# Silu, the key map and the final state on ScalarE, requests a tile ahead and fewer stored halves in a hybrid short-convolution / HGRN2 layer

## The chip, the cores and the metric

The kernel runs on one core of a Trainium2 chip. The metric is the device time of one execution in microseconds. PE is TensorE (matmuls), ACT is ScalarE, DVE is VectorE, POOL is GpSimd and SP is the engine whose queue issues most DMAs (GpSimd's queue issues the rest). In the code they are `T`, `A`, `V`, `G` and `SP`.

## The reference, cut to what matters

One layer runs over a prompt of 2048 tokens and a sample of 64, 1024 features each, in fp32.

```python
h = rms_norm(x, g_pre)
vA, bA, cA, zA, q, f, iv, zB, gA, gB = split_cols(einsum('btd,dn->btn', h, w_in))
u = cA * vA                                             # path A
yA = (silu(zA) * bA * causal_conv3(u, conv_w)) @ w_a_out
fg = lb + (1 - lb) * sigmoid(f)                         # path B: 8 heads of 128
logf, kk, qq = log(fg), 1 - fg, silu(q) * QK_SCALE
S_new, o = hgrn2_scan(S0, qq, kk, iv, logf)             # chunks of 64 tokens
o = o * rsqrt(mean(o * o) + EPS) * g_onorm
yB = (o * silu(zB)) @ w_b_out
out = (sigmoid(gA) * yA + sigmoid(gB) * yB) @ w_o
x = x + rms_norm(out, g_post)
gate = sigmoid(rms_norm(x, g_ple) @ w_ple_gate)
x = x + (p @ w_ple_proj) * gate
```

The outputs are x for both runs, the last two columns of u (the convolution's history) and the final state of each head.

## The kernel before, in words

The 2112 tokens (prompt, sample inside it, prompt) are cut into three blocks of 704 columns; a half is 352 columns. Activations lie with features on the 128 partitions, so one tile is 128 x 704. `rt()` hands out such tiles from a ring of 52, `hf()` tiles of half the width from 9.

Every product is made of three matmuls of 128 x 128 by 352 columns: an operand is split into a high half `hi`, made by a cast on ScalarE, and a low half `lo`, made by a subtraction on VectorE (`split`, L183), and hi·hi, hi·lo and lo·hi are added in PSUM. Weights come from `w_blk` in halves of 256 KB: `load_raw` (L192) asks SP's queue for one, `split_w` (L209) makes `hi` (4 buffers) and `lo`. In the first use of a weight the low half is stored to DRAM (L221); later uses load it (L215) and make only `hi` anew. `load_w` (L224) does this for the two halves of a 1024 x 128 weight column group. Groups 80 to 87 are W_A (`w_a_out`), 88 to 95 W_B, 96 to 103 W_O, 104 to 111 W_G (`w_ple_gate`).

Most of the input projection goes through `sgroup` (L343): two column groups at once by seven block products instead of eight (a Strassen scheme, table at L67), each product 12 matmuls (L357 to L359), in PSUM banks a, c, d, b from a pool of 5. Copies (L371), additions (L377, L382) and a caller's `sink` empty the banks; a sink's `whole` (L391, addition at L396) and `into` (L399, addition at L403) join two partial results. The banks are used again by the next group, so PE waits where a bank's last reader is late.

The stages of a block:

- Path B: for each head `head_prep` (L809) makes forget gates, queries, decays, keys, values and `z` from two `sgroup` calls. `sink_f` stores the sigmoid of f in `sf` and the queries in `qe`. Then come a sigmoid of the queries (L824), the logarithm (L826), the query product (L827), the key map 1 - fg (L828), the scan, and, inside the second group, `scaled`: three exponentials (L840 to L842) and the products with them (L843 to L857). `sink_v` (L859) makes `vt` and `z`. `head_attn` (L873) does the attention of a head; its steps run as hooks between the products of later groups. L942 scales the state at the end of a run.
- Gates, and path A: `path_a` (L751), with `sink_z` for silu(zA) · the rest.
- Merge: block 0 in `merge` (L1048), by `gemm` over `load_w` column groups; blocks 1 and 2 in `merge_in_turn` (L1082), which walks block products over all groups. It names `anew=("A11", "A12")` for W_A and W_B, so of `w_blk` only the second half of groups 4 to 7 (block A22) uses a stored low half there; `out_in_turn` (L1129) has `anew=()` for W_O.
- Final: `final_out`, `final_norm` (L1141; squares L632/L633, column sums on PE L614, transposes L598, x_fm loads L1153), then the gate. `final_gate` (L1185) runs for blocks 0 and 1, inside the first stage of block 1 and the last stage of block 2. It multiplies W_G group j, reloads the tiles `x` and `p` which were put away in DRAM (`reload`, L1041, on POOL's queue), takes the sigmoid (L1191), multiplies and adds (L1192, L1193) and stores y_fm (L1194). Block 2 uses `gate_in_turn` (L1209) at the very end.

A scheduler sets the order of instructions on each engine from the written order, priorities (`tc.high_priority`) and `tc.issue_after`; each engine then executes in that order, and POOL issues its DMAs in order among its other work. In the profile the groups of instructions are named by line, and L184 is the `split` of whatever calls it.

Of the kernel before, what the change touches and what calls it, by code (L numbers as in the profile page):

```python
# [23 lines left out]
CH = 64  # L24
# [58 lines left out]
def hybrid_step(  # L83
# [140 lines left out]
    def load_w(idx, anew=False):  # L224

        parts = []
        for half_ in range(2):
            raw = load_raw(w_blk[idx, half_])
            with tc.high_priority():
                parts.append(split_w(raw, None if anew else (idx, half_)))  # L230
        return parts
# [156 lines left out]
    def half(t, h):  # L388
        return t[:, h * HN : (h + 1) * HN]
# [361 lines left out]
    def path_a(bl, hc, a, first, extra, ready=None):  # L751

        for j in range(KB):
# [36 lines left out]
            def sink_z(c, h, x, y):  # L790
                if c == 1:
                    into(half(b, h), x, y)
                else:
                    v = whole(x, y)
                    A.activation(half(z, h), v, AF.Sigmoid)
                    V.tensor_tensor(half(z, h), v, half(z, h), ALU.mult)

# [11 lines left out]
    def head_prep(bl, hc, hd, first, hs):  # L809
        n, npair = bl["n"], bl["npair"]  # L810
        nch, np1 = n // CH, npair * P
        sf, qe, sq = rt(), rt(), rt()

# [8 lines left out]
        else:  # L822
            sgroup(FF * 8 + hd, QQ * 8 + hd, hc, sink_f, first)
        A.activation(sq, qe, AF.Sigmoid)  # L824
        lg, b, eq = rt(), rt(), rt()
        A.activation(lg, sf, AF.Ln, bias=lb[:, hd : hd + 1], scale=omlb[:, hd : hd + 1])  # L826
        V.scalar_tensor_tensor(qe, qe, QK_SCALE, sq, ALU.mult, ALU.mult)  # L827
        V.tensor_scalar(sf, sf, nomlb[:, hd : hd + 1], omlb[:, hd : hd + 1], ALU.mult, ALU.add)  # L828
        V.tensor_tensor_scan(b, keep[:, :n], lg, 0.0, ALU.mult, ALU.add)
# [6 lines left out]
        def scaled(after):  # L836


            with tc.issue_after(after):
                A.activation(r, ref.rearrange("p c o -> p (c o)"), AF.Exp)  # L840
                A.activation(eq, lg, AF.Exp)
                A.activation(lg, lg, AF.Exp, scale=-1.0)  # L842
            V.tensor_tensor(f[:, 1:nch], r[:, 1:nch], chunks(eq)[:, : nch - 1, CH - 1], ALU.mult)  # L843
# [11 lines left out]
            V.tensor_tensor(f2, f2, f1, ALU.mult)  # L855
            V.tensor_tensor(qe, qe, eq, ALU.mult)
            V.tensor_tensor(chunks(qx), chunks(qe), f.unsqueeze(2).to_broadcast([P, nch, CH]), ALU.mult)  # L857

        def sink_v(c, h, x, y):  # L859
            if c == 1:  # L860
                into(half(vt, h), x, y)
            else:
                v = whole(x, y)
                A.activation(half(z, h), v, AF.Sigmoid)
                V.tensor_tensor(half(z, h), v, half(z, h), ALU.mult)

# [6 lines left out]
    def head_attn(ip, gs, d, hd):  # L873
# [335 lines left out]
    def gate_in_turn(bl, h2, xo, kept):  # L1209

        def sink(g, c, h, x, y):
# [4 lines left out]
            V.tensor_tensor(gate, gate, half(kept["p", j], h), ALU.mult)  # L1216
            (G if c else V).tensor_tensor(gate, gate, half(xo[j], h), ALU.add)
            o = bl["t0"] + h * HN
# [250 lines left out]
```

## Time and profile before

| | us |
|---|---|
| median of 3 runs | 2661.24 (2660.55 to 2661.79) |
| profiled execution, its own time | 2666.81 |
| its span | 2665.0 |
| PE busy | 2615.9 |
| DVE busy | 1755.8 |
| ACT busy | 1461.1 |
| POOL busy | 393.6 |
| mean granted TensorE clock | 0.994 of full speed |

A row of the timeline has the start in us, the duration, engine, line, operation, `output<-inputs` and shape; in brackets the idle time of the engine before it and what ended that. A row of groups has a count, the busy time in us and the mean in ns, and the idle time before. A row of waits reads "waiting instruction <- what released it: us in total, times, longest". A row of a windows view gives, for a stretch, the busy time (and count) of PE, PE's weight loads, DVE, ACT and POOL, then the granted clock, the DMA share and GB/s. A wait is put down to the releaser that came last.

### The profile page before, as it was taken

Reading aid. Unit: us, or ns where it says so; the run is one execution under the profiler, and the core shown is the slowest. Engines: PE = TensorE matmul, PEld = TensorE weight load, DVE = VectorE, ACT = ScalarE, POOL = GpSimd, SP = SyncE. Lnnn points to the kernel's source line nnn. Section 1 sums busy time; section 2 is a strip of 40 time slices with the busy share of each in tenths; the row PEclk is TensorE's granted clock in tenths of the full one; section 3 lists DMA queues with packets and bytes.
Section 4 is the critical chain, followed back from the end, with each engine's and each line's share of the span. In section 5 each row is a group of like instructions: output and inputs, shape, how many; then the busy total and the mean of one; then the engine's idle time right before and its main releaser. Section 6 shows DMA issues by size and latency. Waiting matters only on the chain.

```text
span 2665.0 us, 47847 instructions
## 1 busy us (share of the span) xinstructions
PE 2615.9 (98%) x16646; PEld 2591.9 (97%) x16646; DVE 1755.8 (66%) x3397; ACT 1461.1 (55%) x2818; POOL 393.6 (15%) x721
## 2 busy tenths in 40 slices
PE   7999999999999999999999999999999999999988
PEld 7999999999999999999999999999999999999988
DVE  7688888898667544566645578554466545579746
ACT  5655655454334544566645556456566645565636
POOL 1000000110432111011112211021000101210222
PEclk9999999999999999999999999999999999999999
DMA  8677677898997987766689988599766689989966
GB/s 298 214 257 276 241 259 275 294 319 289 351 354 280 338 298 272 265 220 224 224 278 357 391 305 307 183 350 345 229 224 218 222 256 343 380 307 308 320 234 232
DMA packets 368369, 755.45 MB, mean 283 GB/s; under 512 B 45216, under 2 KB 49856, under 8 KB 368128
## 3 DMA queue, kind: packets, MB, share of 16 engines
q1 hardware_dynamic: 326016, 590.30, 64.4%
q0 software_dynamic: 41824, 162.06, 16.8%
q8 instruction: 131, 2.15, 0.3%
q14 instruction: 110, 0.90, 0.1%
q10 hardware_dynamic: 288, 0.05, 0.0%
HBM read 534.88 MB, written 217.33 MB: 282 GB/s over the span
## 4 chain that ended last, share of the span: by engine, by line
PE 85%; DMA 5%; issue 4%; DVE 4%; ACT 1%; POOL 1%; SPq 0%; DVEq 0%; ACTq 0%; POOLq 0%
PE pg L357 19%; PE pg L359 19%; PE pg L358 19%; PE pg L490 4%; PE pg L491 4%; PE pg L492 4%; PE pg L525 3%; PE pg L524 3%; PE pg L523 3%; DMA low<-s 1%; PE pa L957 1%; PE pa L921 1%; PE pa L911 1%; PE pa L959 1%; PE pa L910 1%
## 5 line engine op out<-in xcount | busy, mean ns | idle before, releaser
L357 PE MATMUL pg<-r,hi 128*128 128x352 f32 x3304 | 1094.9, 332 | 7.9 <-DVE r L403 3.3
L358 PE MATMUL pg<-r,hi 128*128 128x352 f32 x3304 | 1069.1, 324 | 0.0
L359 PE MATMUL pg<-r,lo 128*128 128x352 f32 x2356 | 763.6, 324 | 1.8 <-DMA lo<-low 1.8
L214 ACT CAST hi<-raw 128x512 fp32r<-128x512 f32 x720 | 442.8, 619 | 550.9 <-PE pg L358 194.9
L357 PEld LDWEIGHTS pg<-r,hi 128*128 128x128 f32 x3304 | 623.5, 189 | 14.6 <-issue 6.4
L358 PEld LDWEIGHTS pg<-r,hi 128*128 128x128 f32 x3304 | 624.0, 189 | 0.0
L359 PEld LDWEIGHTS pg<-r,lo 128*128 128x128 f32 x2356 | 443.7, 188 | 2.4 <-DMA lo<-low 2.4
L359 PE MATMUL pg<-r,s 128*128 128x352 f32 x948 | 307.3, 324 | 1.5 <-DMA s<-low 1.5
L523 PE MATMUL pg<-r,hi 128*128 128x352 f32 x768 | 250.4, 327 | 3.4 <-ACT r L184 2.1
L524 PE MATMUL pg<-r,hi 128*128 128x352 f32 x768 | 250.1, 326 | 0.7 <-DVE r L184 0.5
L184 DVE TENSOR_TENSOR r<-r,r 128x352 fp32r<-128x352 f32 (+3 forms) x298 | 183.3, 637 | 62.5 <-ACT r L184 61.7
L491 PE MATMUL pg<-r,hi 128*128 128x352 f32 x672 | 217.4, 325 | 0.1
L525 PE MATMUL pg<-r,lo 128*128 128x352 f32 x656 | 213.3, 325 | 0.5 <-DVE lo L184 0.2
L490 PE MATMUL pg<-r,hi 128*128 128x352 f32 x672 | 213.6, 325 | 0.1
L184 ACT CAST hi<-raw 128x512 fp32r<-128x512 f32 x218 | 133.7, 619 | 143.7 <-PE pg L358 49.7
L184 ACT CAST r<-r 128x352 fp32r<-128x352 f32 (+3 forms) x298 | 161.9, 578 | 70.8 <-DVE r L666 19.0
L184 DVE TENSOR_TENSOR lo<-raw,hi 128x512 fp32r<-128x512 f32 x218 | 148.7, 687 | 58.2 <-ACT hi L184 49.2
L184 ACT CAST hi<-s 128x512 fp32r<-128x512 f32 x160 | 99.0, 619 | 151.9 <-PE pg L358 130.7
L359 PEld LDWEIGHTS pg<-r,s 128*128 128x128 f32 x948 | 178.8, 189 | 2.0 <-DMA s<-low 2.0
L371 ACT COPY hf<-pg 128x352 f32<-128x352 f32 x354 | 156.2, 447 | 6.9 <-PE pg L359 6.3
L523 PEld LDWEIGHTS pg<-r,hi 128*128 128x128 f32 x768 | 145.7, 190 | 5.2 <-ACT r L184 3.0
L524 PEld LDWEIGHTS pg<-r,hi 128*128 128x128 f32 x768 | 145.9, 190 | 1.4 <-DVE r L184 1.4
(366 smaller groups left out, 4234.7 us busy)
## 6 DMA issues: line engine op xcount, KB each, us to landing
raw<-w_blk SPq DMA_DIRECT2D x570, 256.0 KB, 4.2
lo<-low SPq DMA_DIRECT2D x411, 256.0 KB, 4.3
raw<-S SPq DMA_DIRECT2D x408, 256.0 KB, 4.2
low<-lo SPq DMA_DIRECT2D x346, 256.0 KB, 3.7
s<-low SPq DMA_DIRECT2D x309, 256.0 KB, 4.2
S<-s SPq DMA_DIRECT2D x160, 256.0 KB, 3.3
r<-w_blk POOLq DMA_DIRECT2D x64, 256.0 KB, 7.5
S<-r POOLq DMA_DIRECT2D x64, 256.0 KB, 6.3
```

Of the source, the lines that this page charges most:

```text
L184: return A.copy(hi, src).ins, V.tensor_tensor(lo, src, hi.bitcast(F32), ALU.subtract).ins
L214: A.copy(hi, raw)
L357: add(hi[:, k, :], xhi, start=start and k == 0, stop=False)
L358: add(hi[:, k, :], xlo, start=False, stop=False)
L359: last[0] = add(lo[:, k, :], xhi, start=False, stop=k == KH - 1).ins
L371: copied = A.copy(got[n], ps[bank])
L490: add(hi[:, k, :], xhi, start=start and k == 0, stop=False)
L491: add(hi[:, k, :], xlo, start=False, stop=False)
L492: last[0] = add(lo[:, k, :], xhi, start=False, stop=k == KH - 1).ins
L523: T.matmul(ps, hi[:, k % 4, :], xhi[:, c], start=k == ks[0], stop=False)
L524: T.matmul(ps, hi[:, k % 4, :], xlo[:, c], start=False, stop=False)
L525: last[0] = T.matmul(ps, lo[:, k % 4, :], xhi[:, c], start=False, stop=k == ks[-1]).ins
```

## The change

Six edits, called by their place:

1. `final_gate` asks for x and p of tile j + 1 when it begins tile j (`fetch`, `nxt`).
2. `z` in `path_a` and `head_prep`: one Silu on ScalarE in place of a Sigmoid there and a product on VectorE (L796, L865). Queries: the Sigmoid L824 and the VectorE product L827 go; a Silu stands behind the exponentials, and the factor `QK_SCALE` moves into the query product in `scaled` (L856 before).
3. The key map L828 becomes an Identity activation with bias and scale pointers.
4. The final state L942 becomes a multiplication on ScalarE.
5. `load_w` does not store low halves of W_A and W_B and W_O groups 0 to 3 of 8, and not the first half of groups 4 to 7.
6. The last addition of `gate_in_turn` is always on VectorE.

```diff
-                parts.append(split_w(raw, None if anew else (idx, half_)))
+                unread = W_A <= idx < W_O and (idx % KB < KH or half_ == 0)
+                parts.append(split_w(raw, None if anew or unread else (idx, half_)))
...
-                    v = whole(x, y)
-                    A.activation(half(z, h), v, AF.Sigmoid)
-                    V.tensor_tensor(half(z, h), v, half(z, h), ALU.mult)
+                    A.activation(half(z, h), whole(x, y), AF.Silu)
...
-        A.activation(sq, qe, AF.Sigmoid)
         lg, b, eq = rt(), rt(), rt()
         A.activation(lg, sf, AF.Ln, bias=lb[:, hd : hd + 1], scale=omlb[:, hd : hd + 1])
-        V.scalar_tensor_tensor(qe, qe, QK_SCALE, sq, ALU.mult, ALU.mult)
-        V.tensor_scalar(sf, sf, nomlb[:, hd : hd + 1], omlb[:, hd : hd + 1], ALU.mult, ALU.add)
+        A.activation(sf, sf, AF.Identity, bias=omlb[:, hd : hd + 1], scale=nomlb[:, hd : hd + 1])
...
-                A.activation(lg, lg, AF.Exp, scale=-1.0)
+                exps = A.activation(lg, lg, AF.Exp, scale=-1.0).ins
+            with tc.issue_after(exps):
+                A.activation(qe, qe, AF.Silu)
...
-            V.tensor_tensor(qe, qe, eq, ALU.mult)
+            V.scalar_tensor_tensor(qe, qe, QK_SCALE, eq, ALU.mult, ALU.mult)
...
-            V.tensor_scalar(end, cur, d["eq"][:, c * CH + CH - 1 : c * CH + CH], None, ALU.mult)
+            A.mul(end, cur, d["eq"][:, c * CH + CH - 1 : c * CH + CH])
...
+        def fetch(j):
+            return [reload(kept[kind, j]) for kind in "xp"] if j < KB else None
+
+        nxt = fetch(0)
         for j in range(KB):
             pss = gemm(W_G + j, h2, segs)
-            xj, pj = reload(kept["x", j]), reload(kept["p", j])
+            (xj, pj), nxt = nxt, fetch(j + 1)
...
-            (G if c else V).tensor_tensor(gate, gate, half(xo[j], h), ALU.add)
+            V.tensor_tensor(gate, gate, half(xo[j], h), ALU.add)
```

In the built program PE has the same 15569 rows, DVE 3163 instead of 3331, ACT 2872 instead of 2790 (100 table loads instead of 74), POOL 714 instead of 722 and SP 2238 instead of 2262. Lines after the change differ by a few numbers: L865 has no successor, the Silu of `sink_v` is L862, of the queries L841, L403 is L404, L857 is L856, L1043 is L1040, L1153 is L1150, L1194 is L1195.

DVE in a head of block 0, inside the group of zB and iv. `r_1418` (before) and `r_1411` (after) are qx, `r_1420` is z, `hf_1500` and `hf_1493` hold a partial result, L184 and L291 are weight work, L973 is the output norm of the previous head. Before:

```order
L377 TENSOR_TENSOR hf_1500<-hf_1500,pg_1562 128x352
L184 TENSOR_TENSOR lo_1666<-s_1661,hi_1665 128x512
L857 TENSOR_TENSOR r_1418<-r_1154,qc_1415 128x704
L291 TENSOR_TENSOR s_1827<-raw_1813,raw_1815 128x512
L973 SCALAR_TENSOR_TENSOR r_971<-pa_1576,vec,r_971 128x512
L865 TENSOR_TENSOR r_1420<-pg_1487,r_1420 128x352
L184 TENSOR_TENSOR lo_1676<-s_1671,hi_1675 128x512
L184 TENSOR_TENSOR lo_1682<-raw_1643,hi_1681 128x512
L291 TENSOR_TENSOR s_1837<-raw_1815,raw_1817 128x512
L973 SCALAR_TENSOR_TENSOR r_971<-pa_1596,vec,r_971 128x128
L403 TENSOR_TENSOR r_1419<-hf_1500,pg_1512 128x352
```

And after:

```order
L855 SCALAR_TENSOR_TENSOR r_1150<-r_1150,r_1403 128x704
L184 TENSOR_TENSOR lo_1658<-s_1653,hi_1657 128x512
L292 TENSOR_TENSOR s_1685<-raw_1635,s_1663 128x512
L292 TENSOR_TENSOR s_1818<-raw_1804,raw_1806 128x512
L856 TENSOR_TENSOR r_1411<-r_1150,qc_1408 128x704
L184 TENSOR_TENSOR lo_1668<-s_1663,hi_1667 128x512
L970 SCALAR_TENSOR_TENSOR r_968<-pa_1589,vec,r_968 128x128
L292 TENSOR_TENSOR s_1828<-raw_1806,raw_1808 128x512
L184 TENSOR_TENSOR lo_1674<-raw_1635,hi_1673 128x512
L404 TENSOR_TENSOR r_1412<-hf_1493,pg_1505 128x352
```

L865 is gone from the stretch before L403 (L404 after), and the addition L377 into the partial result no longer stands in it.

ACT in a later head of block 0, from the exponentials on (`qc` is the small tile of decays; the last row of each is the activation for z). Before:

```order
L840 ACT_TABLE_LOAD
L840 ACTIVATE qc_2072<-r_2065 128x11
L841 ACTIVATE r_2066<-r_2064 128x704
L842 ACTIVATE r_2064<-r_2064 128x704
L184 CAST hi_2302<-raw_2294 128x512
L184 CAST hi_2312<-s_2308 128x512
L184 CAST hi_2322<-s_2318 128x512
L864 ACT_TABLE_LOAD
L864 ACTIVATE r_2077<-pg_2144 128x352
```

And after:

```order
L837 ACT_TABLE_LOAD
L837 ACTIVATE qc_2061<-r_2055 128x11
L838 ACTIVATE r_2056<-r_2054 128x704
L839 ACTIVATE r_2054<-r_2054 128x704
L184 CAST hi_2290<-raw_2282 128x512
L841 ACT_TABLE_LOAD
L841 ACTIVATE r_1803<-r_1803 128x704
L184 CAST hi_2300<-s_2296 128x512
L184 CAST hi_2310<-s_2306 128x512
L184 CAST hi_2320<-s_2316 128x512
L862 ACTIVATE r_2066<-pg_2133 128x352
```

A table load and the queries' Silu now stand behind the first of the casts; the activation for z has no table load of its own any more.

POOL in the last stage of block 2, where block 1's `final_gate` runs among the norm of block 2. L587 (L588) is a power for the norm, `x_22201` and the like are x tiles put away, `p_442` and the like p tiles. Before:

```order
L1153 DMA r_31148<-x_fm 128x352
L1153 DMA r_31150<-x_fm 128x352
L587 TENSOR_TENSOR cols_31153<-cols_31153,mhalf 128x3
L1043 DMA r_31159<-x_22201 128x704
L1043 DMA r_31161<-p_442 128x704
L587 TENSOR_TENSOR cols_31207<-cols_31207,mhalf 128x3
L1043 DMA r_31248<-x_22238 128x704
L1043 DMA r_31250<-p_486 128x704
L1153 DMA r_31299<-x_fm 128x352
L1194 DMA y_fm<-r_31163 128x704
L1153 DMA r_31332<-x_fm 128x352
L1043 DMA r_31337<-x_22322 128x704
```

And after:

```order
L588 TENSOR_TENSOR cols_30965<-cols_30965,mhalf 128x3
L1150 DMA r_30960<-x_fm 128x352
L1150 DMA r_30962<-x_fm 128x352
L1040 DMA r_30971<-x_22094 128x704
L1040 DMA r_30973<-p_486 128x704
L588 TENSOR_TENSOR cols_31019<-cols_31019,mhalf 128x3
L1040 DMA r_31060<-x_22178 128x704
L1040 DMA r_31062<-p_538 128x704
L1195 DMA y_fm<-r_30975 128x704
L1150 DMA r_31111<-x_fm 128x352
L1195 DMA y_fm<-r_31064 128x704
L1150 DMA r_31144<-x_fm 128x352
```

x and p of a tile are asked for a tile sooner; the x_fm pair that stood ahead of the first power stands behind it, and the next x_fm load behind the first store of y_fm. On PE nine matmuls of W_G move ahead of the second norm's column sums (L614).

More of the change, by code (lines that the diff above doesn't have):

```diff
@@ L811, in head_prep @@
         nch, np1 = n // CH, npair * P
-        sf, qe, sq = rt(), rt(), rt()
+        sf, qe = rt(), rt()
         def sink_f(c, h, x, y):
@@ L862, in sink_v @@
             else:
-                v = whole(x, y)
-                A.activation(half(z, h), v, AF.Sigmoid)
-                V.tensor_tensor(half(z, h), v, half(z, h), ALU.mult)
+                A.activation(half(z, h), whole(x, y), AF.Silu)
         sgroup(ZB * 8 + hd, IV * 8 + hd, hc, sink_v, first, mid=scaled)
```

## The prediction

> **What bounds the kernel now.** I read the page first: span, busy time, chain.
>
> ```profile
> span 2665.0 us, 47847 instructions
> PE 2615.9 (98%) x16646; PEld 2591.9 (97%) x16646; DVE 1755.8 (66%) x3397; ACT 1461.1 (55%) x2818; POOL 393.6 (15%) x721
> ```
>
> TensorE is busy for 2615.9 of 2665.0 us (2615.9 / 16646: a matmul every 0.16 us), and the change removes no matmul. So it can win only inside the 49.1 us in which PE is idle, plus stretches where PE is busy but slow. The profiled run took 2666.81 us, 5.57 above the median of 2661.24; I take gains from its rows and subtract them from the median. About 0.2% (5.3 us) is what a measurement of this kernel can tell from no change.
>
> Next, the waits of PE by releaser (total us, times, longest).
>
> ```profile
> PE pa L614 <- DVE r L633: 9.4, 3, 6.9
> ...
> PE pg L357 <- DVE r L403: 3.3, 8, 0.6
> PE pg L357 <- DVE r L865: 2.5, 7, 0.4
> ...
> PE pa L901 <- DVE r L403: 1.5, 1, 1.5
> ```
>
> Each of these ends on VectorE or ScalarE, which the change lightens or reorders. Each is priced at its place.
>
> **Silu on ScalarE: the heads of block 0.** The timeline at one head boundary, first PE, then VectorE, then ScalarE:
>
> ```profile
> 140.77 0.32 PE L359 MATMUL pg<-r,lo 128*128 128x352 f32 x1
> 141.44 0.42 PE L357 MATMUL pg<-r,hi 128*128 128x352 f32 x1 [0.34 <-DVE r L865]
> 143.32 0.32 PE L359 MATMUL pg<-r,lo 128*128 128x352 f32 x1
> 144.02 0.40 PE L357 MATMUL pg<-r,hi 128*128 128x352 f32 x1 [0.38 <-DVE r L403]
> 133.49 0.88 DVE L852 TENSOR_TENSOR r<-r,r 128x704 f32<-128x704 f32 x1
> 140.86 0.52 DVE L865 TENSOR_TENSOR r<-pg,r 128x352 f32<-128x352 f32 x1
> 143.36 0.52 DVE L403 TENSOR_TENSOR r<-hf,pg 128x352 f32<-128x352 f32 x1
> 132.03 0.79 ACT L842 ACTIVATE r<-r 128x704 f32<-128x704 f32 x1
> 135.04 0.62 ACT L184 CAST hi<-s 128x512 fp32r<-128x512 f32 x1 [1.19 <-PE pg L358]
> 136.98 0.47 ACT L864 ACTIVATE r<-pg 128x352 f32<-128x352 f32 x1
> ```
>
> Two steps from one matmul to the next take 0.67 and 0.70 here instead of 0.16. The first matmul of the next group needs PSUM bank a, which L865 still reads; the third product's needs bank c, which L403 reads. The excess is 0.51 + 0.54 = 1.05 us per head. Seven waits of L865 stand in the list, so 7 × 1.05 = 7.35.
>
> After the change bank a is read last by the Silu on ScalarE, which stands where L864 stands (136.98, ending 137.45): 3.5 us before L865 ends now. For bank c, VectorE must be earlier. From L852 to L403 it runs back to back for 9.87 us. The edit takes L865 (0.43 net of overlap) out of that stretch and, by the order, one L377 (0.43) ahead of it. Also L852 starts 0.67 after the exponential L842 ended (132.82); VectorE was late by work ahead of it, L827 and L828 among it:
>
> ```profile
> L827 DVE SCALAR_TENSOR_TENSOR r<-r,r 128x704 f32<-128x704 f32 x24 | 21.4, 892 | 1.7 <-ACT r L824 1.7
> L828 DVE TENSOR_SCALAR r<-r,lbt 128x704 f32<-128x704 f32 x24 | 15.3, 639 | 7.0 <-ACT r L826 7.0
> L826 ACT ACTIVATE r<-r,lbt 128x704 f32<-128x704 f32 x24 | 23.4, 976 | 0.3
> L840 ACT ACT_TABLE_LOAD x24 | 30.8, 1283 | 0.4
> ```
>
> Without those 0.89 + 0.64 us L852 can start between 0 and 0.67 sooner, so L403 comes 0.43 + 0.43 = 0.86 to 1.53 earlier, against 0.54 needed. I take 7.0 of 7.35. Lower end: only bank a's waits go (7 × 0.51 = 3.6). Upper end 7.35.
>
> The first head has its own wait: L901, 1.5 us on L403. PE's order now puts six other matmuls (6 × 0.16 = 0.97) ahead of those transposes. I take 1.0; ends 0 and 1.5.
>
> The cost on ScalarE: the key map becomes an Identity activation (nearest row L826, a pointer-fed activation: 24 × 0.976 = 23.4), the final state an A.mul (32 small ones, under 0.5 each by L864), 26 more table loads (26 × 1.283 = 33.4). A Silu does not occur in the trace; I price it as the Sigmoid that it replaces, 0.79 whole and 0.47 half, and its upper end by L826, 0.98. That is at most some 75 us on an engine busy for 1461 of 2665. What hides it: PE needs from ScalarE the casts of weights, and four hi buffers stand ahead of PE. A cast may come as late as three products (3 × 12 × 0.16 = 5.8 us) after its buffer is freed. At the head above, the second cast behind the exponentials now stands behind a table load and the queries' Silu (1.28 + 0.79); it comes about 2.1 later than its present 133.24 and ends near 136.0. The cast after it waits for PE until 135.04 and buffers come free a product (1.94) apart, so its own came free at about 133.1; PE wants it at 138.9. 2.9 us of cover are left; I charge 0 (if the cover were gone, each us more would cost PE a us).
>
> **Silu in path A, blocks 1 and 2.** L796 leaves VectorE in the same way. PE waits there at two places for L377 and L403:
>
> ```profile
> 2280.74 0.40 PE L357 MATMUL pg<-r,hi 128*128 128x352 f32 x1 [0.56 <-DVE hf L377]
> 2283.54 0.40 PE L357 MATMUL pg<-r,hi 128*128 128x352 f32 x1 [0.61 <-DVE r L403]
> ```
>
> L796 is the same operation as L865 (0.52), about the size of each wait. I take 1.0; ends 0 and 1.2.
>
> **Low halves not stored.** The merge of block 0 issues 24 stores of 256 KB fewer.
>
> The waits of PE from 700 to 870 us, and a cast on ScalarE there:
>
> ```profile
> PE pg L523 <- ACT hi L184: 1.1, 2, 0.6
> PE pg L523 <- ACT r L184: 0.7, 1, 0.7
> ```
>
> ```profile
> 746.11 0.62 ACT L184 CAST s<-r 128x512 fp32r<-128x512 f32 x1 [4.02 <-DMA low<-s]
> ```
>
> That cast of a prepared sum waits 4.02 for an earlier store to leave its buffer; the weight cast behind it comes late, and PE waits. Fewer stores empty the queues sooner. The two rows of waits hold 1.8 us; I take 1.0, about half, since the stores of sums remain; ends 0 and 1.8. No later block reads these halves, so nothing is split again for their lack.
>
> **Requests a tile ahead: the last W_G stage of block 1.** The largest single wait. Rows of the timeline (PE, VectorE, POOL), VectorE's waits from 2528 to 2560 us in sums, and how long the x_fm loads took to land:
>
> ```profile
> 2559.84 1.41 PE L614 MATMUL pa<-ones,r 128*128 128x1 f32 x6 [6.91 <-DVE r L633]
> 2529.88 0.52 DVE L1163 TENSOR_TENSOR r<-r,r 128x352 f32<-128x352 f32 x1
> 2512.43 1.08 POOL L1153 DMA_DIRECT2D r<-x_fm  x2 [2.27 <-PE pg L492]
> 2525.24 0.89 POOL L587 TENSOR_TENSOR cols<-cols,mhalf 128x3 f32<-128x3 f32 x1 [11.73 <-DVE cols L585]
> ```
>
> ```profile
> DVE r L1192 <- DMA r<-p: 6.0, 3, 4.0
> DVE r L1163 <- DMA r<-x_fm: 0.8, 1, 0.8
> ```
>
> ```profile
> DMA to landing us min/median/max: 4.6/5.5/8.1
> ```
>
> VectorE stood 6.0 + 0.8 = 6.8 us in loads, 4.01 of it at once, and the squares L633 on which PE waits come behind them. With p requested a tile (48 matmuls, 7.7 us) ahead, its three waits go. But POOL issues in order, and in its new order the x_fm loads stand later. The pair requested before L587 at 2512 now comes after it (2526.1) and lands 5.5 later, 2531.6; its first reader L1163 could start at 2529.9: a new wait of 1.7. The next x_fm load now stands behind the first y_fm store. Adding up the durations of VectorE's rows in the new order, that store is issued at 2535.1, the load at 2535.6; it lands at 2541.1 and is wanted at 2539.2: 1.9. So VectorE waits 3.6 where it waited 6.8, and the squares end 3.2 earlier. In the new order PE also reaches L614 nine matmuls (1.45) later. The stall becomes 6.91 − 3.2 − 1.45 = 2.3: a gain of 4.6.
>
> Behind the stall the granted clock is low (columns: PE, PEld, DVE, ACT, POOL, clock, DMA share, GB/s):
>
> ```profile
> 2561.10:2565.70 4.60, 4.60 (x17) 4.60 (x18) 1.87 (x3) 0.00 (x0) 3.42 (x5) 0.50 0.20 78
> 2565.70:2570.30 4.60, 4.60 (x31) 4.57 (x30) 2.69 (x6) 1.09 (x2) 0.79 (x2) 0.98 0.89 306
> 935.00:937.00 2.00, 2.00 (x9) 2.00 (x8) 0.00 (x0) 0.38 (x1) 0.05 (x1) 0.50 1.04 414
> ...
> 932.26 1.47 PE L614 MATMUL pa<-ones,r 128*128 128x1 f32 x12 [0.89 <-DVE r L633]
> ```
>
> In 4.60 us PE starts 17 matmuls where the next 4.60 us have 31: 14 × 0.16 = 2.2 us lost. The same 0.50 stands at 935, after a wait of only 0.89, so a shorter stall need not save it; I take half, 1.1. The Trainium skill, "TensorE: Matmul & The Clock Gate", Part 1, says that the clock falls to half after an idle window of about 3.4 us. By that rule a stall of 2.3 keeps the clock, the gain is 2.2 rather than 1.1, and the sum gives 2642.2; the row at 935 does not bear it out.
>
> This stage: 4.6 + 1.1 = 5.7. Ends: if the two x_fm loads take the longest landing, 8.1, each wait is 2.6 longer, and the stall becomes 7.5 (−0.6); if they are hidden and the clock holds, 6.91 + 2.2 = 9.1.
>
> **The tail.** In the last gate VectorE adds what POOL added.
>
> ```profile
> 2657.11 0.32 PE L492 MATMUL pg<-r,lo 128*128 128x352 f32 x1
> 2661.35 0.52 DVE L1217 TENSOR_TENSOR hf<-hf,r 128x352 f32<-128x352 f32 x1
> 2650.91 1.27 DVE L511 TENSOR_TENSOR r<-r,hf 128x352 f32<-128x352 f32 x1
> 2660.27 0.50 ACT L1215 ACTIVATE hf<-hf 128x352 f32<-128x352 f32 x1 [1.64 <-DVE hf L396]
> ```
>
> From PE's end (2657.43) to VectorE's (2661.87) are 4.4 us, though the work is one addition L396, a Sigmoid 0.50, a product and an addition of 0.52 each: 2.1 with L396 at 0.52, some 2.2 with the steps between. A VectorE addition of 0.52 elsewhere takes 1.27 at 2650.91, while POOL adds beside it, and such operations pile up. Without POOL I take 2.2. The eight additions cost VectorE 8 × 0.52 = 4.2 over the stage. Ends: 0, if they make the pile instead, and 2.4.
>
> **Sum**: 7.0 + 1.0 + 0 + 1.0 + 1.0 + 5.7 + 2.2 = 17.9. From 2661.24 that is 2643.3; against the profile's own time, 2648.9. All lower ends: 3.6 + 0 + 0 + 0 + 0 − 0.6 + 0 = 3.0, so 2658.2; all upper ends: 7.35 + 1.5 + 1.2 + 1.8 + 9.1 + 2.4 = 23.4, so 2637.8.
>
> **Rivals.**
> ScalarE becomes the bound (slower). It issues in order, so a table load and a Silu hold up every cast behind them. It decides once a cast at a head comes more than the 2.9 us of cover later than I worked out; each us beyond costs PE 1 us in 24 heads. At 3.9 later the heads lose 24, and the time is 2667.3. For it: the Silu and its table switches are unmeasured. Against it: casts now wait for PE to free buffers, not the reverse; table loads in the trace have 0.4 us of idle before all 24, and L842 and its neighbours follow each other without a gap. The Trainium skill, "ScalarE: Activation LUTs", section "What ACT_TABLE_LOAD costs", adds about 1.38 us of drain to the 1.283 of each load; the 1283 agrees with the row, the drain does not show in it. By the page the two loads at a head would take 2.76 of the 2.9. Chance 0.11.
>
> The last W_G stage keeps its stall: x_fm loads at their longest put the waits back, −0.6 instead of 5.7: 2649.6. For it: 8.1 has occurred. Against: the median is 5.5. Chance 0.15.
>
> Only bank a's wait goes, and L403 stays late (VectorE fills the room with other queued work): 3.6 instead of 7.0: 2646.7. For it: VectorE is busy without a break there. Chance 0.12.
>
> Nothing reaches PE: each wait passes to the next releaser, and the terms come out at their lower ends, or POOL's and ScalarE's delays eat the rest: 2656 to 2666. For it: PE is 98% busy, and many inputs are needed within 1 us of each other. Chance 0.07.
>
> **How the numbers follow.** My forecast (2637.8 to about 2650) has 0.55. It and the two partial rivals (0.15, 0.12) lie below 2655.9: faster 0.82. No effect: 0.07. ScalarE as the bound: 0.11. The range leaves out the slower case and no effect (0.18) and 0.02 below: 2635 to 2655.9.
>
> **What would show it.** Right: in block 0 no PE wait on the Silu's line, and those on L404 (now L403) below 1 us in all; the L614 wait near 2555 at about 2 us, with VectorE waiting for x_fm instead of p; no weight cast waiting 3 us behind an activation; PE's end to the last VectorE instruction at about 2.2 us. Wrong: waits of PE on hi L184 or hi L214 growing at the heads (ScalarE), a stall over 6 at L614, or L404 still releasing PE 0.5 at each head.

## The result, and the profile after

The changed kernel takes 2642.98 us (median of 4 runs, 2639.34 to 2644.82), the kernel before 2661.51 us (4 runs, 2660.55 to 2662.33): a ratio of 0.9929, 95% interval 0.9912 to 0.9946, so 18.5 us faster. The forecast was 2643.3. That the sum came out does not mean that each term did; the traces show which.

The page of the changed kernel, span, busy time and chain:

```profile
span 2643.1 us, 47577 instructions
PE 2609.3 (99%) x16646; PEld 2591.5 (98%) x16646; DVE 1679.8 (64%) x3229; ACT 1525.5 (58%) x2900; POOL 387.0 (15%) x713
```

PE's idle time fell from 49.1 to 33.8 us, and its busy time for the same matmuls by 6.6. Most of the 6.6 belongs to that one trace of before: in a second one (below) PE is busy for 2610.2 us and idle for 44.0. VectorE gave up 76 us, ScalarE took on 64.

PE's waits by releaser in the changed kernel (a few rows; those of L1017 and L429 are its start, which before had 7.7 and 2.3 there):

```profile
PE pa L1017 <- ACT r L184: 6.7, 1, 6.7
PE pa L615 <- DVE r L634: 5.8, 3, 2.0
...
PE pg L429 <- DVE r L184: 3.1, 1, 3.1
PE pg L360 <- DMA lo<-low: 2.1, 2, 1.9
PE pg L358 <- DVE r L404: 1.8, 7, 0.6
```

The stall of 6.91 is gone (the longest at L615 is 2.0), the late reader L865 is gone, and L404 (L403 before) still has seven waits, six of them of 0.2 and one of 0.6. Waits for the loads `lo<-low` are about what they were (2.1 after 1.8), but one stands at a new place, 1061 us.

The other two of the three stalls at L615 grew. They are the column sums near 920 and 1775 us (timeline of PE):

```profile
919.66 1.47 PE L615 MATMUL pa<-ones,r 128*128 128x1 f32 x12 [2.00 <-DVE r L634]
1775.49 1.68 PE L615 MATMUL pa<-ones,r 128*128 128x1 f32 x9 [2.00 <-DVE r L634]
```

Before they were 0.89 and 1.65, in a second trace of before 1.04 and 0.90; in a second trace of the changed kernel they are 1.95 and 1.98. The prediction has no term for this.

The same place in the last W_G stage, where PE stood 6.91 us and VectorE 4.01 for p (timeline of PE, VectorE and two rows of POOL):

```profile
2542.47 0.80 PE L615 MATMUL pa<-ones,r 128*128 128x1 f32 x6 [1.78 <-DVE r L634]
...
2527.04 0.53 DVE L1160 TENSOR_TENSOR r<-r,r 128x352 f32<-128x352 f32 x1 [2.01 <-DMA r<-x_fm]
...
2521.08 0.54 POOL L1195 DMA_DIRECT2D y_fm<-r  x1 [3.60 <-issue]
2521.61 0.55 POOL L1150 DMA_DIRECT2D r<-x_fm  x1
```

VectorE no longer waits for p. It waits 2.01 us for the x_fm load that stands behind the first y_fm store on POOL's queue, and PE stalls for 1.78; just ahead of the end of that stall VectorE's last square (L634) also waits 0.62 for ScalarE's L633. After this stall, too, the clock is low (a windows view):

```profile
2544.00:2548.00 4.00, 4.00 (x19) 3.93 (x17) 1.62 (x3) 0.00 (x0) 3.24 (x6) 0.59 0.37 138
```

To see where the time went, I took the start of the n-th matmul of the block products (there are 14,424) in each trace, subtracted it from the start of the same matmul in the first trace of before, and read how much that difference rises in each stretch. The stretches are named by times in the first trace of before; a positive number is time gained there, "end" is what follows the last matmul. The last column is the difference of the spans, 2665.0 less the span. The other rows are the experiments below.

| us gained in | to 100 | 100-112.5 first head | 112.5-690 heads, path A | 690-870 merge | 870-1050 | 1050-1085 | 1085-1650 | 1650-1800 | 1800-2500 | 2500-2650 last W_G | end | span |
|---|---|---|---|---|---|---|---|---|---|---|---|---|
| after | -1.3 | 1.7 | 5.9 | 5.4 | 2.2 | -3.4 | -0.6 | 2.5 | 1.2 | 6.5 | 1.8 | 21.9 |
| after_again | -1.0 | 0.3 | 5.9 | 5.4 | 1.0 | -1.5 | -0.5 | 5.1 | 1.1 | 4.9 | 1.8 | 22.4 |
| before_again | 1.1 | 1.1 | 0.0 | 3.4 | 1.3 | 0.1 | -0.3 | 3.8 | 0.9 | -0.5 | 0.0 | 10.8 |
| silu_undone | 0.5 | 1.2 | 0.1 | 5.2 | 0.2 | 0.4 | -1.0 | 3.8 | 1.4 | 8.8 | 1.7 | 22.3 |
| zb_undone | 0.1 | 1.7 | -3.5 | 5.4 | 0.3 | -1.0 | -2.4 | 3.8 | 1.1 | 6.4 | 1.8 | 13.7 |
| keymap_dve | 1.4 | 1.8 | 2.0 | 5.4 | 0.7 | -2.1 | -0.6 | 2.9 | 1.1 | 7.1 | 1.8 | 21.4 |
| silu_early | 1.6 | 1.3 | -6.2 | 5.5 | -0.3 | -0.1 | -3.2 | 3.3 | -0.4 | 8.1 | 1.7 | 11.5 |
| no_fetch | 1.6 | 1.7 | 5.9 | 5.4 | 1.2 | -1.5 | -1.4 | 2.6 | 0.9 | 2.2 | 1.8 | 20.4 |
| stores_kept | 1.7 | 1.7 | 5.2 | 4.6 | -0.8 | -2.4 | -0.6 | 3.1 | 0.5 | 7.0 | 1.4 | 21.4 |
| pool_add | 1.9 | 1.7 | 5.7 | 4.6 | 0.6 | -1.6 | -0.6 | 3.9 | 1.3 | 6.2 | 0.6 | 24.3 |
| xfm4 | 0.9 | 0.3 | 5.9 | 5.1 | 0.6 | -1.8 | -0.6 | 6.4 | 1.3 | 9.6 | 1.8 | 29.5 |
| xfm4_early0 | 1.9 | 1.7 | 6.0 | 5.4 | 1.1 | -0.2 | -1.1 | 2.2 | 1.0 | 9.8 | 1.8 | 29.5 |
| xfm4_silu_undone | 1.0 | 0.0 | 0.1 | 5.0 | 0.5 | -1.2 | 0.1 | 5.0 | 1.2 | 9.7 | 1.8 | 23.3 |

One trace is one execution, and the stretches that wait for DMAs scatter by 2 to 4 us from one to the next. Where a column hardly scatters among kernels with the same code there (112.5 to 690: 5.2 to 6.0 in the seven that have all edits of the heads in their places), a single trace is enough; elsewhere it is not.

### The profile page after: what moved, and what is told of

It reads as the page before. It is cut to its first block, busy times and chain, and to the rows that moved or that the text cites. A ratio compares the mean times of both kernels' runs of the same rounds, so it can differ in the third digit from the quotient of the medians.

```text
span 2643.1 us, 47577 instructions
## 1 busy us (share of the span) xinstructions
PE 2609.3 (99%) x16646; PEld 2591.5 (98%) x16646; DVE 1679.8 (64%) x3229; ACT 1525.5 (58%) x2900; POOL 387.0 (15%) x713
## 4 chain that ended last, share of the span: by engine, by line
PE 90%; DMA 4%; DVE 3%; issue 2%; ACT 1%; POOL 0%; SPq 0%; ACTq 0%; DVEq 0%; POOLq 0%
PE pg L358 19%; PE pg L360 18%; PE pg L359 18%; PE pg L526 4%; PE pg L525 4%; PE pg L524 4%; PE pg L491 4%; PE pg L492 4%; PE pg L493 4%; PE pa L918 1%; PE pa L954 1%; PE pa L908 1%; PE pa L956 1%; DMA raw<-S 1%; PE pa L907 1%
## 5 line engine op out<-in xcount | busy, mean ns | idle before, releaser
L184 DVE TENSOR_TENSOR r<-r,r 128x352 fp32r<-128x352 f32 (+3 forms) x298 | 183.1, 636 | 63.8 <-ACT r L184 63.1
L184 ACT CAST hi<-raw 128x512 fp32r<-128x512 f32 x218 | 134.4, 619 | 151.6 <-PE pg L359 45.1
L184 ACT CAST r<-r 128x352 fp32r<-128x352 f32 (+3 forms) x298 | 162.0, 579 | 59.2 <-DVE r L667 15.0
L184 DVE TENSOR_TENSOR lo<-raw,hi 128x512 fp32r<-128x512 f32 x218 | 149.2, 685 | 68.0 <-ACT hi L184 52.3
L184 ACT CAST hi<-s 128x512 fp32r<-128x512 f32 x160 | 98.0, 618 | 122.2 <-PE pg L359 106.4
L372 ACT COPY hf<-pg 128x352 f32<-128x352 f32 x354 | 157.1, 446 | 12.1 <-PE pg L360 11.5
```

The lines of the kernel that those rows point to most:

```text
L184: return A.copy(hi, src).ins, V.tensor_tensor(lo, src, hi.bitcast(F32), ALU.subtract).ins
L372: copied = A.copy(got[n], ps[bank])
```

## The experiments

The times of before drifted between sets of runs (medians 2656.5 to 2661.5), so each variant is judged by its ratio to the kernel before, run on the same chip. The half widths of the intervals are 0.0009 to 0.0017 of the time, 2.4 to 4.5 us: where the intervals of two variants overlap, only the traces tell them apart.

| kernel | median us | ratio to before, 95% interval |
|---|---|---|
| after (the result) | 2642.98 | 0.9929, 0.9912 to 0.9946 |
| after_again | 2644.32 | 0.9945, 0.9932 to 0.9959 |
| before_again | 2658.10 | 0.9996, 0.9985 to 1.0006 |
| stores_kept | 2645.31 | 0.9958, 0.9946 to 0.9970 |
| no_fetch | 2648.02 | 0.9966, 0.9954 to 0.9978 |
| silu_undone | 2644.32 | 0.9959, 0.9945 to 0.9972 |
| pool_add | 2644.00 | 0.9954, 0.9941 to 0.9967 |
| zb_undone | 2654.31 | 0.9979, 0.9970 to 0.9988 |
| keymap_dve | 2647.66 | 0.9957, 0.9945 to 0.9969 |
| silu_early | 2658.51 | 0.9998, 0.9989 to 1.0007 |
| xfm4 | 2640.49 | 0.9931, 0.9919 to 0.9944 |
| xfm4_early0 | 2638.49 | 0.9925, 0.9913 to 0.9938 |
| xfm4_silu_undone | 2646.02 | 0.9951, 0.9937 to 0.9964 |

### A second trace of each kernel

`before_again` and `after_again` are the two kernels without an edit.

> The kernel before, unchanged, for a second trace of it. In four variants of the changed kernel, with each edit undone in turn, PE has no wait over 0.2 us between 730 and 860 us, where the first trace of before lost 5.4 us. Theory 'one trace': that stall belongs to that one execution and not to the kernel; the new trace has less than 1 us of waits there and a span of some 2655 to 2658. Rival 'two edits together': the waits come from the kernel before and any of the edits cures them; then some 2.7 us of waits on L184 and L1121 stand there again.

> The changed kernel, unchanged, for a second trace of it and a comparison with the undone variants. Expected 2641 to 2645. If the loss of 3.4 us at 1060 us (a load of a low half late by 1.9, then half the clock) belongs to the edits on ScalarE, it stands here again, since it stood in all traces that have these edits and not in the one without; if it was a chance of one execution it may be gone.

PE's waits of the second trace of before, from 700 to 860 us:

```profile
PE pg L523 <- ACT hi L184: 0.5, 1, 0.5
PE pg L525 <- DVE lo L184: 0.2, 1, 0.2
```

Here the merge has 0.7 us of waits where the first trace had 2.7 and lost more. So 3.4 of the 5.4 us that the merge seems to gain belong to that first execution, and so do the 3.8 between 1650 and 1800 and about 0.9 between 1800 and 2500. The first trace of before was simply a long one: its span is 10.8 us longer than the second's. What stands in both are the heads (0.0 between the two), the stall at the column sums (6.91 and 7.02) and the end (7.6 us after the last matmul in both).

### Is it the stores?

```diff
-                unread = W_A <= idx < W_O and (idx % KB < KH or half_ == 0)
-                parts.append(split_w(raw, None if anew or unread else (idx, half_)))
+                parts.append(split_w(raw, None if anew else (idx, half_)))
```

> The changed kernel with the 24 low halves stored again (edit 5 undone alone). Aligned matmul by matmul, the two traces differ by 5.4 us between 740 and 870 us, in the merge of block 0. Theory 'stores': the fewer stores free SP's queue and the buffers there, so that gain goes back: 2643 + 5.4 = about 2648, with PE waits of some 2.5 us on L184 between 730 and 870 us again. Rival 'shift': the merge gained because path B ended earlier and its loads met other traffic; then the time stays near 2643 and the merge has no PE wait over 0.5 us.

With the stores back PE has no wait at all listed between 700 and 860 us, and the merge gains 4.6 against 5.4: the stores are worth at most 0.8 us there, and pool_add, which leaves them out, has 4.6 too. What ScalarE waits there for earlier stores, by trace (690 to 870 us; before, before_again, stores_kept, after):

```profile
ACT s L184 <- DMA low<-s: 23.6, 9, 7.5
ACT s L184 <- DMA low<-s: 25.8, 10, 6.7
ACT s L184 <- DMA low<-s: 23.5, 11, 6.7
ACT s L184 <- DMA low<-s: 15.4, 9, 6.3
```

ScalarE waits less in the changed kernel, but PE does not feel it: stores_kept has the long waits and no wait of PE. (They are 24.5 in silu_undone, which leaves the stores out, so the fewer stores alone do not shorten them.) The ratio (0.9958 against 0.9945 for after_again) leaves room for nothing as well as for some 8 us over the whole kernel; what edit 5 gives beyond the merge is not settled. The expected 5.4 fell: it had been read from one execution.

### Is it the requests?

```diff
-        nxt = fetch(0)
...
-            (xj, pj), nxt = nxt, fetch(j + 1)
+            xj, pj = fetch(j)
```

> The changed kernel with x and p asked for in their own tile again (edit 1 undone alone). Theory 'requests': the stall of PE at the last column sums of block 1 is 6 to 7 us again instead of 1.8, with VectorE waiting 4 us for p, and the time is 2643 + 6.4 = about 2649. Rival 'order': nine matmuls more ahead of the column sums and the earlier VectorE work made the gain, so the stall is below 4 us and the time below 2646.

The waits of VectorE (2510 to 2545 us) and of PE in this variant:

```profile
DVE r L1192 <- DMA r<-p: 3.5, 2, 2.2
...
DVE r L1160 <- DMA r<-x_fm: 1.7, 1, 1.7
```

```profile
2541.61 1.41 PE L615 MATMUL pa<-ones,r 128*128 128x1 f32 x6 [5.09 <-DVE r L634]
```

VectorE waits for p again and PE stalls 5.09. The stage gains 2.2 us against 6.5 and 4.9: edit 1 is worth 2.7 to 4.3 us. That holds more than the loads: the nine matmuls go back too (these column sums stand behind 13,945 of the counted matmuls in before and here, behind 13,954 in the changed kernel). So neither theory is alone right, and the two parts of edit 1 were not tested apart. The stall is 5.09 instead of 6.91 though PE's place is that of before; this rest comes with VectorE's other work there. By the ratios edit 1 is worth 0.0021, 5.6 us, with intervals that overlap.

### The next thing late in that stage

```diff
-        for _ in range(2 if bl["last"] else 4):
+        for _ in range(4):
```

> The changed kernel with four x_fm tiles instead of two asked for ahead in the last block's norm. In the changed kernel VectorE waits 2.0 us for the third x_fm load, which stands behind a store of y_fm on GpSimd's queue, and PE then stalls 1.8 us at the column sums and runs at half clock for some 3 us. Theory: the x_fm wait is what is late next; without it the stall is below 0.5 us, and 1.8 + about 1.5 come off: about 2640. Rival: another wait of VectorE takes its place (x_fm loads further back, or the sigmoid of tile 3), the stall stays at 1 to 2 us and the time at 2643.

From 2500 to 2600 us PE has no wait listed any more; VectorE has none for a load. The stage gains 9.6 instead of 6.5 and 4.9, and the median falls by 3.8 us against after_again in the same set of runs (the intervals of the ratios overlap, so the size is the trace's). The x_fm load was what was late next, as the prediction's working had it.

### Which edit frees the heads?

Three variants: all edits on ScalarE undone (the code of before at those places, in path A too), the z of the heads alone, and the key map alone. The z of the heads:

```diff
-                A.activation(half(z, h), whole(x, y), AF.Silu)
+                v = whole(x, y)
+                A.activation(half(z, h), v, AF.Sigmoid)
+                V.tensor_tensor(half(z, h), v, half(z, h), ALU.mult)
```

The whole undoing has, beside this and the key map, the queries and the final state:

```diff
+        A.activation(sq, qe, AF.Sigmoid)
...
+        V.scalar_tensor_tensor(qe, qe, QK_SCALE, sq, ALU.mult, ALU.mult)
...
-            with tc.issue_after(exps):
-                A.activation(qe, qe, AF.Silu)
...
-            A.mul(end, cur, d["eq"][:, c * CH + CH - 1 : c * CH + CH])
+            V.tensor_scalar(end, cur, d["eq"][:, c * CH + CH - 1 : c * CH + CH], None, ALU.mult)
```

And the key map:

```diff
-        A.activation(sf, sf, AF.Identity, bias=omlb[:, hd : hd + 1], scale=nomlb[:, hd : hd + 1])
+        V.tensor_scalar(sf, sf, nomlb[:, hd : hd + 1], omlb[:, hd : hd + 1], ALU.mult, ALU.add)
```

> The changed kernel with edits 2, 3 and 4 undone: Sigmoid and product for z and queries, key map and final state on VectorE again; edits 1, 5 and 6 stay. Theory 'bank readers': the heads of block 0 wait again at both banks (seven times about 0.9 us), the first head about 1.3 more, path A of block 2 about 1.1: 2643 + 8.7 = about 2652. Rival 'ScalarE pays': the 65 us more on ScalarE cost something elsewhere that undoing gives back, so the time is below 2649.

> The changed kernel with only the z of the heads undone: Sigmoid on ScalarE and a product on VectorE again (L865 of before); all else stays. Theory 'bank readers': that product is the late reader of bank a, so at the head boundaries of block 0 PE waits for it again; the trace before had 0.34 idle and 0.51 excess at seven places, so the heads gain 5.9 - 3.6 = about 2.3 us instead of 5.9, and the time is 2643.5 + 3.6 = about 2647. Rival 'VectorE load': any 0.5 us less of VectorE work at a head would do; the key map and the queries' product still gone make room, bank a is free in time, and the time stays at 2643 to 2645.

> The changed kernel with only the key map back on VectorE (0.64 us each, 24 times). In the changed kernel PE still waits 0.20 us for bank c at six head boundaries, so the room that the working gave VectorE there (some 0.3 to 1.0 us) is used up. Theory 'no room': the key map's 0.64 comes on top of the 0.2 at the heads of block 0, some 0.3 to 0.6 us each, 2 to 4 us in all: 2645.5 to 2647.5. Rival 'hidden': the key map runs well ahead of the products that PE waits for, the wait stays 0.2, and ScalarE's 0.98 us less per head gives nothing or up to 1 us back: 2642 to 2644.

PE's waits from 112 to 450 us, first in the changed kernel, then with z undone, then with the key map undone:

```profile
PE pg L358 <- DVE r L404: 1.2, 6, 0.2
```

```profile
PE pg L358 <- DVE r L864: 10.6, 7, 1.5
```

```profile
PE pg L358 <- DVE r L404: 5.2, 7, 0.8
```

With z undone the product on VectorE holds bank a for 1.5 us at every boundary, more than the two waits of before together (0.34 and 0.38), and bank c then has no wait: the heads lose 3.5 us against before instead of gaining 5.9. Why it comes out later here than in before was not tested; the order of VectorE around it is another one. With the key map on VectorE bank c is late by 0.75 each, and 3.9 of the 5.9 us are lost. Both theories of a late reader hold for the place of the wait. For z the price was missed: 2654.3 against the expected 2647, since a misplaced reader costs more than the wait seen before suggested. With everything undone the heads gain 0.1: the 5.9 us are the edits' own.

Yet silu_undone was no slower than the changed kernel (2644.32, by ratio 0.9959 against 0.9945), 8 us from what was expected. Its last W_G stage gained 8.8 instead of 4.9 to 7.0, it has no wait at 1060 us (below), and its stalls at the two earlier column sums (near 920 and 1775 us in the changed kernel) are 0.84 and 0.90 instead of 2.0 each. To take the last stage out, the same edit was made on top of four x_fm tiles:

> Four x_fm tiles ahead, with edits 2, 3 and 4 undone (Sigmoids and products on VectorE again). The edits on ScalarE gained 5.9 us in the heads of block 0, yet the variant with them undone was as fast as the changed kernel: 2644.3 against 2643.0 and 2644.3, with 8.8 us instead of 4.9 to 7.0 gained in the last W_G stage. Here the stall of that stage is gone for both. Theory 'worth 4': the heads' 5.9 less about 2 lost at 1060 us remain, the last stage was chance: 2640.5 + 4 = about 2644.5. Rival 'worth nothing': ScalarE's load gives all of it back elsewhere, some place other than 1060 us: 2640 to 2641.

2646.0 against 2640.5 for xfm4 (ratio 0.9951 against 0.9931, 5.3 us, with intervals that just overlap; the spans of the two traces differ by 6.2): the edits on ScalarE are worth some 4 to 6 us. That the good result of silu_undone in the last stage was chance, as that of after_again (4.9) in the other direction, is likely but not shown: it is one trace.

### What the edits cost on ScalarE

```diff
+        A.activation(qe, qe, AF.Silu)
         lg, b, eq = rt(), rt(), rt()
...
-                exps = A.activation(lg, lg, AF.Exp, scale=-1.0).ins
-            with tc.issue_after(exps):
-                A.activation(qe, qe, AF.Silu)
+                A.activation(lg, lg, AF.Exp, scale=-1.0)
```

> The changed kernel with the queries' Silu moved ahead of the logarithm, where the Sigmoid stood before: 147 table loads instead of 100 (47 x 1.283 = 60 us more on ScalarE), but no table load and Silu between the exponentials and the casts. Theory 'cover': ScalarE has room at the heads, so the heads of block 0 keep their 5.8 us gain, and the wait at 1060 us goes: 2643 - 3.4 = about 2640. Rival 'ScalarE is the bound': a microsecond for each of 24 heads, 2643 + 24 = about 2667, with PE waits on casts at the heads.

47 more table loads, 60 us on an engine that is busy 58% of the time, cost 14.2 us against after_again: 2658.5 (ratios 0.9998 and 0.9945, far apart). PE's waits from 112 to 450 us, and one of them with ScalarE and VectorE ahead of it:

```profile
PE pa L967 <- DVE one L962: 7.7, 7, 1.2
PE pg L358 <- DVE hf L378: 3.3, 7, 0.5
```

```profile
229.61 1.28 ACT L838 ACT_TABLE_LOAD   x1
230.91 0.22 ACT L838 ACTIVATE qc<-r 128x11 f32<-128x11 f32 x1
231.03 0.78 ACT L839 ACTIVATE r<-r 128x704 f32<-128x704 f32 x1
231.72 0.60 ACT L184 CAST hi<-raw 128x512 fp32r<-128x512 f32 x1
...
232.35 0.69 DVE L184 TENSOR_TENSOR lo<-raw,hi 128x512 fp32r<-128x512 f32 x1 [0.57 <-ACT hi L184]
232.96 0.28 DVE L962 TENSOR_TENSOR one<-pa,ms 128x128 f32<-128x128 f32 x1
...
233.39 0.30 PE L967 MATMUL pa<-ident,one 128*128 128x128 f32 x1 [1.09 <-DVE one L962]
```

PE does not wait for the late cast itself. VectorE does, since its subtraction L184 stands ahead of the small product L962 for which PE waits 1.09. So both sides fell in part: there is no room of microseconds at the heads, and it is not a microsecond for each of 24 heads either. The seven heads of block 0 pay 12.1 us (5.9 and 6.2 the other way), the rest of the path some 4 (the columns 1085 to 1650 and 1800 to 2500).

The changed kernel itself pays in one place, at the first head of block 1, whose weight sums are made anew. PE, ScalarE ahead of it, and the clock behind it:

```profile
1061.40 0.43 PE L360 MATMUL pg<-r,lo 128*128 128x352 f32 x1 [1.87 <-DMA lo<-low]
```

```profile
1046.26 1.28 ACT L841 ACT_TABLE_LOAD   x1
1047.55 0.79 ACT L841 ACTIVATE r<-r 128x704 f32<-128x704 f32 x1
1048.25 1.13 ACT L184 CAST hi<-s 128x512 fp32r<-128x512 f32 x2
```

```profile
1062.00:1066.00 4.00, 4.00 (x17) 4.00 (x17) 0.52 (x1) 1.41 (x2) 0.53 (x1) 0.57 0.95 329
```

The casts of the new sums stand behind the table load and the Silu; SP's queue stores the low halves made from them in order, and the loads that PE wants are issued behind these stores. To test whether the place of the Silu matters, the Silu of that one head alone was moved ahead of the logarithm, on top of four x_fm tiles:

```diff
+        early = hd == 0 and not hs and bl["t0"] == BN
+        if early:
+            A.activation(qe, qe, AF.Silu)
...
+            if not early:
+                with tc.issue_after(exps):
+                    A.activation(qe, qe, AF.Silu)
```

> Four x_fm tiles ahead (2640.5 before) and the queries' Silu ahead of the logarithm in the first head of block 1 alone, where the Silu and its table load behind the exponentials are followed by casts of weight sums made anew. Theory: ScalarE is late there, the stores of low halves wait for it on SP's queue and hold up the loads behind them, which is the wait of 1.5 to 2.4 us at 1060 us and half the clock after it; moved, 1.5 to 3 us come off: 2637.5 to 2639. Rival: the wait there comes from the DMA traffic after block 0's gate and not from this Silu; it stays and so does the time, 2640 to 2641.

```profile
PE pg L358 <- DVE r L404: 0.2, 1, 0.2
```

That is all that PE waits for from 1040 to 1090 us in this variant: the load's wait is gone, and the stretch loses 0.2 us instead of 1.0 to 3.4 (all eight traces with the Silu behind the exponentials there have that wait, 1.0 to 2.4 us). A variant with Sigmoids has 0.8 there once, so part of it may come and go.

So the place of the Silu brings the wait. That late stores carry it, as the expectation has it, does not come out. SP's queue from the last store of a low half to the first load `lo<-low` behind it, in the changed kernel and then in xfm4_early0:

```profile
1053.11 0.32 SPq L221 DMA_DIRECT2D low<-lo  x1
...
1056.01 1.60 SPq L215 DMA_DIRECT2D lo<-low  x3
```

```profile
1050.69 0.32 SPq L221 DMA_DIRECT2D low<-lo  x1
...
1051.64 0.41 SPq L215 DMA_DIRECT2D lo<-low  x1
```

PE's matmuls stand 2.14 us later in the changed kernel at that time. Counted from them the store is only 0.28 late (1053.11 - 1050.69 - 2.14), but the load is 2.23 late (1056.01 - 1051.64 - 2.14), about as much as PE waits. With the Silu moved, the program has another order on SP's queue: one load stands between the store and this one, in the changed kernel four do.

The time of xfm4_early0 is 2638.5 us, ratio 0.9925: the lowest median here, ahead of after_again by 0.0020 by the ratios, whose intervals meet, and of the result's 0.9929 by less; against xfm4 (0.9931) the times cannot tell it apart, only the traces.

### The end

```diff
-            V.tensor_tensor(gate, gate, half(xo[j], h), ALU.add)
+            (G if c else V).tensor_tensor(gate, gate, half(xo[j], h), ALU.add)
```

> The changed kernel with the last additions of the gate half on GpSimd again (edit 6 undone alone). Theory: VectorE operations beside GpSimd's additions take 1.2 to 1.8 us instead of 0.52 again, and from the last matmul to the last VectorE instruction it takes 4.4 us instead of 2.7: 2643 + 1.7 = about 2645. Rival: the earlier end comes from elsewhere; VectorE's end stays 2.7 us behind PE, no change in time.

From the last matmul to the end of the span this variant takes 6.94 us, the changed kernel 5.78 twice, before 7.57 and 7.58. So undoing the edit alone gives back 1.2 of the 1.8 us gained at the end, and the rival falls; the median (2644.0) cannot tell this from no change. The last matmul and the last rows of VectorE in the changed kernel:

```profile
2637.00 0.32 PE L493 MATMUL pg<-r,lo 128*128 128x352 f32 x1
```

```profile
2637.80 0.51 DVE L397 TENSOR_TENSOR hf<-r,pg 128x352 f32<-128x352 f32 x1
2638.93 0.52 DVE L1217 TENSOR_TENSOR hf<-hf,r 128x352 f32<-128x352 f32 x1 [0.62 <-ACT hf L1216]
2639.49 0.53 DVE L1218 TENSOR_TENSOR hf<-hf,r 128x352 f32<-128x352 f32 x1
```

VectorE ends 2.7 us after PE, against 4.4. No addition there takes 1.27 any more.

## Why the prediction was right

The larger terms were right in mechanism and nearly in size: heads, last stage and end were forecast at 14.9 together and measured at 13.6. The smaller ones were not: first head, ScalarE, path A and merge were forecast at 3.0 and come to some 0.7. The sum of the measured terms is some 14.3, so that 17.9 met the 18.5 of the result to 0.6 is partly luck.

- Heads of block 0: 7.0 forecast, 5.9 measured in both traces. The mechanism is the one named: bank a's late reader L865 is gone and VectorE is earlier. Short by 1.1, since PE still waits a little for bank c at every boundary. The step that failed is "against 0.54 needed": once PE no longer loses 0.51 at bank a, it comes to bank c that much sooner, so 0.54 + 0.51 = 1.05 was needed. The rows of the changed kernel at that boundary:

```profile
142.16 0.51 DVE L404 TENSOR_TENSOR r<-hf,pg 128x352 f32<-128x352 f32 x1
...
142.26 0.32 PE L360 MATMUL pg<-r,lo 128*128 128x352 f32 x1
142.72 0.43 PE L358 MATMUL pg<-r,hi 128*128 128x352 f32 x1
```

  L403 stood at 143.36, L404 stands 1.20 earlier; the whole trace was ahead by 0.41 there (the sum of the first two columns), so the edits moved it by 0.79, a little less than the 0.86 to 1.53 worked out. 1.05 less 0.79 is 0.26 short, and PE's step is 0.46 instead of 0.16. keymap_dve shows that 0.64 more on VectorE costs 3.9 us.
- First head: 1.0 forecast; 1.7 and 0.3 in the two traces after, 0 and 1.1 in those before, so some 0.5. The wait of the transposes is 1.2 in both traces after (L898 on L404), 1.5 and 1.8 before (L901 on L403): the six matmuls put ahead of them took off only 0.3 to 0.6, not 0.97.
- ScalarE: 0 forecast, about 2 lost at one head, and not by the slower rival's mechanism. The step that failed is the charge of 0 on the cover of 2.9 us: it asked only whether casts reach PE in time, at an ordinary head. At the head where sums are made anew the new place of the Silu came with another order of loads on SP's queue, and PE waits for one of them; and silu_early shows that VectorE, in order behind a cast, is hurt before PE is. The longer stalls at the two earlier column sums come with the same edits (0.84 to 1.70 in the two traces with them undone, 0.89 to 1.65 in the two of before, 1.34 to 2.23 with them); why was not tested, and the columns 870 to 1050 and 1650 to 1800 scatter too much to price them. The rival's 1 us in each of 24 heads did not come in the changed kernel, which has fewer loads than silu_early. The prices were right, by the groups of the changed kernel (count, busy us, mean ns, idle before):

```profile
L841 ACT ACT_TABLE_LOAD x24 | 30.8, 1283 | 0.4
...
L841 ACT ACTIVATE r<-r 128x704 f32<-128x704 f32 x24 | 19.0, 793 | 0.3
```

  Between 24 loads and their Silus lie 0.3 us in all. The drain of 1.38 us a switch that the Trainium skill, "ScalarE: Activation LUTs", section "What ACT_TABLE_LOAD costs", adds does not show here.
- Path A: 1.0 forecast. Both traces after gain 1.1 to 1.2 from 1800 to 2500, and the second trace before gains 0.9: the term is 0.2. The wait on L377 was a thing of that one execution, and the one on L403 stands in all traces (0.6). silu_undone has the same gain, so L796 had nothing to do with it.
- Merge: 1.0 forecast, 5.4 in the table, of which 3.4 are the first trace's; 2.0 remain, and at most 0.8 from the stores. The mechanism failed: the row of 4.02 us was taken for what makes PE wait, but in stores_kept ScalarE waits for earlier stores as long as before and PE does not wait. What the 2.0 come from stays open.
- Last W_G stage: 5.7 forecast, 6.5 and 4.9 measured, on average 5.9 against the mean of both traces before. The new wait for x_fm that was worked out as 1.9 was 2.01, the stall 1.78 for 2.3; the first x_fm wait (1.7 forecast) did not come. The low clock behind the short stall came as taken: half, not nothing.
- End: 2.2 forecast, 1.8 measured.

Against the second trace of before, whose execution took 2656.0 us, 2.1 below the median of its runs, the spans differ by 11.1 and 11.6 us; by the runs the change is worth 14.7 (after_again) to 18.5 us (the result). The forecast of 17.9 lies at the upper side of this.

## What to carry to other kernels

Take a second trace before pricing a wait that appears once: what repeats at every head or stage is the kernel's, what appears once may be the execution's. When work is moved to an engine with 40% idle time, ask what stands in order behind it on that engine and behind its results on the next, and compare the order of the DMA queues too; here 47 more table loads (60 us) cost 14 us, while the changed kernel's 64 us on ScalarE cost PE some 2 at one head, by the order of loads on SP's queue. When a load is asked for earlier on a shared queue, the next load in that queue is what becomes late, and moving that one too took PE's stall there away (3.8 us by the medians, whose intervals overlap).

## What was not expected of the hardware

The clock of TensorE fell to about half after short waits: 0.57 in the window after the 1.87 us wait at 1061 us, 0.59 after the 1.78 us wait at 2542 us. It did not fall in every case: in after_again the wait at the same place ended at 1063.4 after 1.54 us, and the next 4 us have 1.00:

```profile
1063.40:1067.40 4.00, 4.00 (x25) 4.00 (x26) 0.71 (x2) 2.12 (x4) 0.47 (x1) 1.00 1.00 374
```

The Trainium skill, "TensorE: Matmul & The Clock Gate", Part 1, puts the fall behind an idle window of about 3.4 us; these waits are shorter, and the measurement decides. A second thing: two executions of the same kernel differ by 10.8 us in span (2665.0 and 2654.2 for before), spread over several stretches (3.8 from 1650 to 1800 us, 3.4 in the merge); what makes them differ is not known.
